# Loading the context's weights from ScalarE's queue, a unit behind each expert's tanh, and sharing the units out by the experts' rows

## The chip, the cores and the metric

One core of a Trainium2 chip runs one program. The time is that of the device in microseconds (us); the kernel before took 2759.27 us, the median of three runs from 2755.33 to 2763.97.

## The reference

Two models run one after the other on 256 tokens of width 1024, in float32. The first is one layer: attention, then 32 experts of which each token takes four. The second has two layers of attention, gated MLP, convolution and feed-forward, and besides its own tokens it carries a context of 256 tokens through its first layer. Cut to what matters here:

```
def moe_ffn(h, ...):                      # first model
    top_val, top_idx = lax.top_k(h @ w_router + b_router, 4)
    for each expert e and the tokens that chose it:
        gu  = x @ w_gate_up[e] + b_gate_up[e]             # 1024 -> 2048
        g   = minimum(gu[:, :1024], 7); u = clip(gu[:, 1024:], -7, 7)
        act = (u + 1) * (g * sigmoid(1.702 * g))
        y  += gate * (act @ w_down[e] + b_down[e])        # 1024 -> 1024
x = first_block(x, ...)
for l in range(2):                        # second model
    k_all = concatenate([kc, k]); ...     # the latent attends to the context too
    x = layer(x, k_all, v_all)
    if l == 0:
        xc = layer(ctx, kc, vc)           # the context, same weights, needs no x
```

The context's layer reads nothing that the first model computes, so it can be worked on while the experts run.

## The kernel before

**Experts.** An expert has 12.6 MB of weights. They are loaded in tiles of 2 MB, four for `w_gate_up` (L947) and two for `w_down` (L958), by SP's queue, into a ring of three such tiles (`big`, L930ff). The experts have fixed capacities, handed out by load: one of 128 rows, 15 of 64, 16 of 32 (`CAPS`). `GROUPS` sets their order: groups of four of 32 rows and of two of 64 take turns, with the one of 128 in between; from the eighth group on only pairs of 64 are left. For a group the tokens are gathered on PE (L847, into `hG`); for each expert follow the biases (L1036), the up matmuls (L981), `swiglu` (L915ff: clip on VectorE, tanh on ScalarE at L923 into `et`, two products on VectorE into `eg`), the transposes (L987), ScalarE's copy into `aT` (L989), the down matmuls (L1006) and ScalarE's copy into `y` (L1042). The down matmuls of an expert are emitted behind the up matmuls of the next. `combine` spreads a group's result over the tokens (L897, L898; L903 adds it to `xT`).

**The context pass.** `ctx_pass` (L1416ff) is a generator: between two `yield`s it emits about one unit. A unit is one block of weights of 1024 × 512 (2.1 MB, `load_w`, L317ff), fetched in four loads of 512 KB at L330 into three buffers `raws` and, every fourth, `rawx`; eight splits into a high and a low part (ScalarE `whis` L342, VectorE `wlos` L343), and 96 matmuls at L365 into the banks `side`. It ends with a residual (L1728, L1729) and a store of 1 MB to DRAM on GpSimd's queue (`cd`, L1570). While `self.side` is true the tiles are the context's own.

**What sets the order.** A scheduler orders each engine's instructions by priority. `prio` (L1765ff) emits the experts at high priority; after each of their `yield`s it lets `run_ctx(n)` emit n steps of the context at low priority. `MOE` holds these n: one in two of three entries for 22 entries, then one in each. When the context has ended, `self.solo` becomes true, and from there `big` may hand out five more tiles of 1 MB (`SPARE`), which were the context's.

**The seam.** Behind the last expert all engines branch on whether a token was left over (`overflow`, L1070ff; it is not taken here), and the second model's layers begin, with ScalarE's squares of `xT` into `merged` (L238).

Of the kernel before, what the change touches and what calls it, by code (L numbers as in the profile page):

```python
# [14 lines left out]
AF = mybir.ActivationFunctionType  # L15
# [12 lines left out]
CAPS = [128] + [64] * 15 + [32] * 16  # L28
SEQ = list(range(16, 20)) + [1, 2] + list(range(20, 24)) + [3, 4] + list(range(24, 28)) + [0] + list(range(28, 32)) + list(range(5, 16))
GROUPS = [[]]  # L30
# [68 lines left out]
class Builder:  # L99
    def __init__(self, tc, a, out, dbg=None):  # L100
        self.tc, self.nc, self.a, self.out = tc, tc.nc, a, out
        self.dbg = dbg or {}
        self.n = self.slot = self.hslot = 0
        self.side = False
        self.fbg = 0
        self.nblock, self.second = 0, None
        self.firstw = []
        self.after, self.fill = None, deque()
        self.cq = {False: deque(), True: deque()}
        self.cpool, self.cpool_s = CPOOL, CPOOL_S  # L110
        self.bg = deque()
# [204 lines left out]

    def load_w(self, w, q=None):

        q = q or self.nc.sync
        small = self.side  # L320
        if self.tail:
            self.nblock += 1
            small = self.nblock % 3 == 0
        whole = None if small else self.t(self.raw, [P, 4096], tag="raw")
        rows, k0 = [], 0
        for h in (1, 1, 1, 1) if small else (2, 2):
            n = 2 * h
            r = self.half() if small else whole[:, k0 * 512:(k0 + n) * 512]
            r = r.rearrange("p (k n) -> p k n", k=n)
            q.dma_start(r, w[:, k0:k0 + n, :])  # L330
            rows += [r[:, i:i + self.wn, :] for i in range(0, n, self.wn)]
            k0 += n
        return rows
# [583 lines left out]
    def swiglu(self, pool, pg, pu, n):  # L917
        nc = self.nc
        g = self.t(pool, [P, 512], tag="eg", bufs=1)
        nc.vector.tensor_scalar(g[:, :n], pg[:, :n], 7.0, None, op0=OP.min)  # L920
        nc.vector.tensor_scalar(pu[:, :n], pu[:, :n], -7.0, 7.0, op0=OP.max, op1=OP.min)
        th = self.t(pool, [P, 512], tag="et", bufs=1)
        nc.scalar.activation(th[:, :n], g[:, :n], AF.Tanh, scale=0.5 * 1.702)  # L923
        nc.vector.scalar_tensor_tensor(g[:, :n], th[:, :n], 1.0, g[:, :n], op0=OP.add, op1=OP.mult)
        nc.vector.scalar_tensor_tensor(g[:, :n], pu[:, :n], 1.0, g[:, :n], op0=OP.add, op1=OP.mult)
        return g
# [839 lines left out]
    def build(self, stop=None):  # L1766
        tc, a = self.tc, self.a
        with ExitStack() as st:
# [6 lines left out]
            with tc.tile_pool(name="ps1", bufs=1, space=PSUM) as self.psum, \  # L1775
# [5 lines left out]
                def run_ctx(n):  # L1781
                    self.side = True
                    for _ in range(n):
                        if next(ctx, 1):
                            self.solo = True
                            break
                    self.side = False
# [6 lines left out]
                with tc.tile_pool(name="moe", bufs=1) as mp:  # L1794
# [5 lines left out]
                    with tc.tile_pool(name="mw", bufs=1) as self.mw:  # L1800
                        self.prio(self.moe(mp), MOE, run_ctx)
                        run_ctx(100)
# [34 lines left out]
TSLOTS = ("gl", "gate")  # L1837
FRONT = [2, 2, 2, 1, 1, 1, 1, 1, 1, 1, 1, 1, 1, 1, 1, 1, 1, 1]
ROUTE = [1, 0, 0]
MOE = [1 if i % 3 else 0 for i in range(22)] + [1] * 22  # L1840


_BIG = ['w_ada', 'w_in', 'w_out', 'b_router', 'w_gate_up', 'b_gate_up', 'w_down', 'b_down', 'ada_w_2', 'w_in_2',
# [37 lines left out]
```

## Time and profile before

| | |
|---|---|
| median of three runs | 2759.27 us |
| profiled execution, its own time | 2754.71 us |
| its span | 2752.8 us |
| PE busy in the span | 2592.5 us (94%) |
| VectorE / ScalarE / GpSimd busy | 1626.1 / 1157.5 / 322.2 us |
| moved in all | 769.80 MB, mean 280 GB/s |
| first and last tanh of the experts | 349.1 and 1561.7 us |

PE is TensorE's matmul queue, PEld its weight loads, DVE VectorE, ACT ScalarE, POOL GpSimd, SP the engine whose queue issues most loads; a q behind a name is the engine's sequencer, which waits and issues. A row of the table of windows gives a stretch in us from the span's start, its length, then busy us and (x) number of instructions of PE, PEld, DVE, ACT and POOL, the granted clock of PE as a share of full speed, the share of time in which the DMA engines are busy, and GB/s. A row of waits gives who waits (engine, tile, line), for whom, the us in total, how often, and the longest. A row of a timeline gives start, us, engine, line, operation, out<-in, and in brackets how long the engine stood idle before and who released it. Names of weights read as in the program (`in_w_ff_dram` are the feed-forward weights).

### The profile page before, as it was taken

The numbers are of one execution on the slowest core, as the hardware profiler recorded it, in microseconds if no ns is written. First come the engines' busy times: TensorE is split into PE (matmuls) and PEld (weight loads), VectorE is DVE, ScalarE is ACT, GpSimd is POOL, SyncE is SP. The second block draws the span as 40 slices with busy tenths as digits, with TensorE's granted clock in tenths as the row PEclk, the third lists the DMA queues.
The fourth block names the chain that finished last, engine by engine and source line by source line (L and its number), as shares of the span: only waits on it lengthen the run. The fifth ranks groups of instructions, "written<-read, shape, count | busy, mean of one in ns | idle before, by whom it ended". The sixth has DMA issues, their size and how long they took to land. (4 is left out here: it accounts for less than half of the span.)

```text
span 2752.8 us, 49781 instructions
## 1 busy us (share of the span) xinstructions
PE 2592.5 (94%) x20358; PEld 2047.0 (74%) x20359; DVE 1626.1 (59%) x3090; ACT 1157.5 (42%) x1987; POOL 322.2 (12%) x334
## 2 busy tenths in 40 slices
PE   7999999999899999999889978899999998999998
PEld 5657877678567777875333477899789987899998
DVE  3465543778554524443121279988546789996655
ACT  2333343333243323431111156765445566656543
POOL 0000000000000000000000025442001055350000
PEclk9989899999999999999999989999999999999999
DMA  9758599989999999999999934326854443344442
GB/s 398 300 226 296 203 401 417 364 347 405 378 357 386 390 361 361 409 419 363 392 392 421 415 129 168 125 105 238 289 203 184 158 180 123 131 146 184 154 184 85
DMA packets 119370, 769.80 MB, mean 280 GB/s; under 512 B 11632, under 2 KB 12016, under 8 KB 52832
## 3 DMA queue, kind: packets, MB, share of 16 engines
q1 hardware_dynamic: 117744, 759.15, 70.6%
q0 software_dynamic: 1392, 7.41, 0.7%
q8 instruction: 162, 2.65, 0.4%
q14 instruction: 72, 0.59, 0.1%
HBM read 762.84 MB, written 3.67 MB: 278 GB/s over the span
## 5 line engine op out<-in xcount | busy, mean ns | idle before, releaser
L343 DVE TENSOR_TENSOR wlo<-raw,whi 128x1024 fp32r<-128x1024 f32 (+1 forms) x288 | 337.6, 1175 | 162.2 <-ACT whi L342 156.6
L365 PE MATMUL lin<-hhi,wlo 128*128 128x256 f32 x1440 | 399.3, 283 | 21.6 <-DVE wlo L343 21.6
L365 PE MATMUL lin<-hhi,whi 128*128 128x256 f32 x1440 | 400.5, 282 | 2.2 <-ACT hhi L284 2.2
L365 PE MATMUL lin<-hlo,whi 128*128 128x256 f32 x1440 | 401.4, 281 | 0.1
L342 ACT ACTIVATE whi<-raw 128x1024 fp32r<-128x1024 f32 (+1 forms) x288 | 276.9, 963 | 257.9 <-PE lin L365 189.3
L981 PE MATMUL mlin<-raw,hG 128*32 128x256 f32 (+2 forms) x2920 | 341.3, 456 | 17.5 <-DMA raw<-in_w_gate_up_dram 17.5
L365 PEld LDWEIGHTS lin<-hhi,wlo 128*128 128x128 f32 x1440 | 269.5, 190 | 37.5 <-DVE wlo L343 33.2
L1585 POOL TENSOR_TENSOR yc<-yc,ctmp 128x256 f32<-128x256 f32 x240 | 252.4, 1075 | 300.6 <-ACT ctmp L1584 300.1
L343 DVE TENSOR_TENSOR wlos<-raws,whis 128x512 fp32r<-128x512 f32 x246 | 166.2, 687 | 196.3 <-ACT whis L342 189.4
L365 PEld LDWEIGHTS lin<-hhi,whi 128*128 128x128 f32 x1440 | 271.0, 189 | 5.8 <-ACT hhi L284 3.7
L365 PEld LDWEIGHTS lin<-hlo,whi 128*128 128x128 f32 x1440 | 272.2, 189 | 3.7 <-issue 2.3
L981 PEld LDWEIGHTS mlin<-raw,hG 128*32 128x32 f32 (+2 forms) x2920 | 129.9, 121 | 178.6 <-issue 110.0
L342 ACT ACTIVATE whis<-raws 128x512 fp32r<-128x512 f32 x246 | 148.9, 627 | 225.6 <-PE side L365 186.2
L365 PE MATMUL side<-hhi,whis 128*128 128x256 f32 x720 | 203.0, 288 | 0.1
L365 PE MATMUL side<-hlo,whis 128*128 128x256 f32 x720 | 199.7, 282 | 0.0
L365 PE MATMUL side<-hhi,wlos 128*128 128x256 f32 x720 | 193.1, 284 | 0.7 <-DVE wlos L343 0.5
L343 DVE TENSOR_TENSOR wlo<-raws,whi 128x1024 fp32r<-128x1024 f32 x108 | 139.0, 1287 | 74.4 <-ACT whi L342 73.8
L1587 DVE SCALAR_TENSOR_TENSOR yc<-gl,cw,yc 128x256 f32<-128x256 f32 x240 | 167.8, 734 | 0.1
L342 ACT ACTIVATE whi<-raws 128x1024 fp32r<-128x1024 f32 x108 | 114.4, 1059 | 118.8 <-PE lin L365 103.8
L1006 PE MATMUL main<-raw,aT 128*32 128x256 f32 (+2 forms) x1408 | 162.6, 453 | 1.1 <-DMA raw<-in_w_down_dram 1.0
L365 PEld LDWEIGHTS side<-hhi,whis 128*128 128x128 f32 x720 | 136.7, 190 | 16.5 <-issue 11.2
L365 PE MATMUL lin<-ahi,whi 128*128 128x256 f32 x528 | 145.7, 279 | 0.0
(603 smaller groups left out, 5737.4 us busy)
## 6 DMA issues: line engine op xcount, KB each, us to landing
raw<-in_w_gate_up_dram SPq DMA_DIRECT2D x120, 2048.0 KB, 11.5
raw<-in_w_down_dram SPq DMA_DIRECT2D x55, 2048.0 KB, 11.1
raw<-in_w_in_dram SPq DMA_DIRECT2D x60, 1024.0 KB, 7.1
raws<-in_w_in_dram SPq DMA_DIRECT2D x95, 512.0 KB, 6.8
raws<-in_w_ff_dram SPq DMA_DIRECT2D x88, 512.0 KB, 8.1
raw<-in_w_ff_dram SPq DMA_DIRECT2D x44, 1024.0 KB, 7.0
phi<-in_ada_w_dram SPq DMA_DIRECT2D x10, 1024.0 KB, 7.4
plo<-in_ada_w_dram SPq DMA_DIRECT2D x10, 1024.0 KB, 7.1
```

What stands on the lines that cost most here:

```text
L342: x = nc.scalar.activation(flat(hi), flat(rows[i]), AF.Copy)
L343: y = nc.vector.tensor_sub(flat(lo), flat(rows[i]), flat(hi).bitcast(F32))
L365: x = nc.tensor.matmul(*args, skip_group_check=True, **kw)
L981: nc.tensor.matmul(d, hT(k), gu[k][c0 // D][:, c0 % D:c0 % D + W], start=False, stop=(k == KC - 1), skip_group_check=True)
L1006: nc.tensor.matmul(pys[h][g * C:(g + 1) * C, :W], st, dn[m][:, c0:c0 + W], start=(m == 0), stop=(m == KC - 1), skip_group_check=True)
L1585: nc.gpsimd.tensor_add(d, d, m)
L1587: self.paced(1, nc.vector.scalar_tensor_tensor(d, x, wcol, d, op0=OP.mult, op1=OP.add))
```

## The change

The loads of a unit of the context are issued by ScalarE's queue in place of SP's. `swiglu` keeps its tanh in `self.eload`, and the first of a unit's four loads is ordered behind the tanh that was emitted last. `MOE` is computed: each expert earns context steps by its capacity, 1.3 for 32 rows, 0.55 for 64, 0 for 128; a step is handed out when the sum reaches a whole number. What remains is emitted behind the last expert by `run_ctx(100)`. In all 164 loads go to ScalarE's queue, and since the context now ends behind the last expert, `solo` is not true in any expert: the five tiles of 1 MB aren't used for expert weights. Line numbers behind the change are 2 higher.

```diff
--- before.py
+++ after.py
@@ -104,7 +104,7 @@
         self.side = False
         self.fbg = 0
         self.nblock, self.second = 0, None
-        self.firstw = []
+        self.firstw, self.eload = [], None
         self.after, self.fill = None, deque()
         self.cq = {False: deque(), True: deque()}
         self.cpool, self.cpool_s = CPOOL, CPOOL_S
@@ -316,7 +316,7 @@
 
     def load_w(self, w, q=None):
 
-        q = q or self.nc.sync
+        q = q or (self.nc.scalar if self.side else self.nc.sync)
         small = self.side
         if self.tail:
             self.nblock += 1
@@ -327,7 +327,9 @@
             n = 2 * h
             r = self.half() if small else whole[:, k0 * 512:(k0 + n) * 512]
             r = r.rearrange("p (k n) -> p k n", k=n)
-            q.dma_start(r, w[:, k0:k0 + n, :])
+            x = q.dma_start(r, w[:, k0:k0 + n, :])
+            if self.side and self.eload is not None and k0 == 0:
+                self.behind(x, self.eload)
             rows += [r[:, i:i + self.wn, :] for i in range(0, n, self.wn)]
             k0 += n
         return rows
@@ -920,7 +922,7 @@
         nc.vector.tensor_scalar(g[:, :n], pg[:, :n], 7.0, None, op0=OP.min)
         nc.vector.tensor_scalar(pu[:, :n], pu[:, :n], -7.0, 7.0, op0=OP.max, op1=OP.min)
         th = self.t(pool, [P, 512], tag="et", bufs=1)
-        nc.scalar.activation(th[:, :n], g[:, :n], AF.Tanh, scale=0.5 * 1.702)
+        self.eload = nc.scalar.activation(th[:, :n], g[:, :n], AF.Tanh, scale=0.5 * 1.702)
         nc.vector.scalar_tensor_tensor(g[:, :n], th[:, :n], 1.0, g[:, :n], op0=OP.add, op1=OP.mult)
         nc.vector.scalar_tensor_tensor(g[:, :n], pu[:, :n], 1.0, g[:, :n], op0=OP.add, op1=OP.mult)
         return g
@@ -1837,7 +1839,22 @@
 TSLOTS = ("gl", "gate")
 FRONT = [2, 2, 2, 1, 1, 1, 1, 1, 1, 1, 1, 1, 1, 1, 1, 1, 1, 1]
 ROUTE = [1, 0, 0]
-MOE = [1 if i % 3 else 0 for i in range(22)] + [1] * 22
+SHARE = {32: 1.3, 64: 0.55, 128: 0.0}
+
+
+def moe_steps():
+
+
+    steps, due, done = [], 0.0, 0
+    for group in GROUPS:
+        for i in [None] + group:
+            due += SHARE[CAPS[i]] if i is not None else 0.0
+            steps.append(int(due) - done)
+            done = int(due)
+    return steps
+
+
+MOE = moe_steps()
 
 
 _BIG = ['w_ada', 'w_in', 'w_out', 'b_router', 'w_gate_up', 'b_gate_up', 'w_down', 'b_down', 'ada_w_2', 'w_in_2',
```

**ScalarE, among the late experts of 64 rows.** Before, behind the tanh into `et` (L923), only the experts' own copies stand:

```order
L923 ACTIVATE et_12493<-eg_12490 128x512 [waits DVE_49,Activation_49]
L989 ACTIVATE aT_12502<-main_12497 128x512 [waits PE_49]
L1042 ACTIVATE y_11574<-main_12508 64x512 [waits PE_49]
L1042 ACTIVATE y_11574<-main_12508 64x512
L290 ACTIVATE yh_12527<-y_11574,gcol_11572 128x512 [waits Activation_49]
L290 ACTIVATE yh_12545<-y_11574,gcol_11572 128x512 [waits DVE_49,PE_49]
L923 ACTIVATE et_12763<-eg_12760 128x512 [waits DVE_49]
```

Now loads of the context (L330, with the buffers that they fill) and its splits (`whis`) stand between an expert's tanh and its copy into `aT`:

```order
L290 ACTIVATE yh_12929<-y_12432,gcol_12430 128x512 [waits Activation_49]
L290 ACTIVATE yh_12947<-y_12432,gcol_12430 128x512 [waits DVE_49,PE_49]
L925 ACTIVATE et_13025<-eg_13022 128x512 [waits DVE_49]
L330 DMA raws_13061<-in_w_ff_2_dram 128x1024 [waits DMAHW4_49]
L330 DMA raws_13063<-in_w_ff_2_dram 128x1024 [waits DMAHW5_49]
L330 DMA raws_13065<-in_w_ff_2_dram 128x1024 [waits DMAHW6_49]
L991 ACTIVATE aT_13034<-main_13029 128x512 [waits PE_49]
L344 ACTIVATE whis_13071<-raws_13061 128x512 [waits DMAHW4_49]
L344 ACTIVATE whis_13087<-raws_13061 128x512
```

Three loads and, behind the copy into `aT`, the first two splits came in.

**VectorE, behind the last expert.** Before, the last additions of `combine` (L903) stand right ahead of the overflow check (L1070):

```order
L903 SCALAR_TENSOR_TENSOR xT_70<-main_14458,mod_14_97,xT_70 128x256 [waits DVE_49,PE_49]
L903 SCALAR_TENSOR_TENSOR xT_70<-main_14458,mod_14_97,xT_70 128x256 [waits DVE_49]
L903 SCALAR_TENSOR_TENSOR xT_70<-main_14465,mod_14_97,xT_70 128x256 [waits DVE_49,PE_49]
L903 SCALAR_TENSOR_TENSOR xT_70<-main_14465,mod_14_97,xT_70 128x256 [waits DVE_49]
L1070 TENSOR_LOAD ovi_5203 [waits DVE_49,DMASW1_49,PE_49,DMASW3_49,Activation_49,Pool_49]
L1071 COMPARE_AND_BRANCH
```

Now the context's last square root (`rs_`, nine instructions) and its residual into the tile `m` (L1730, L1731) stand between the last addition (L905) and the check (L1072):

```order
L905 SCALAR_TENSOR_TENSOR xT_70<-main_14377,mod_14_97,xT_70 128x256 [waits PE_49]
L905 SCALAR_TENSOR_TENSOR xT_70<-main_14377,mod_14_97,xT_70 128x256
L163 TENSOR_SCALAR rs_vs_14409<-side_14384 128x2 [waits PE_49]
...
L173 SCALAR_TENSOR_TENSOR rs_rs_14411<-rs_ts_14412,rs_rs_14411 128x2 [waits DVE_49]
L1730 SCALAR_TENSOR_TENSOR hks_14424<-y_1727_9377,Lp_208_1035,side_14421 128x256 [waits PE_49]
L1730 SCALAR_TENSOR_TENSOR hks_14427<-y_1727_9377,Lp_208_1035,side_14421 128x256
L1731 TENSOR_TENSOR m_1676_9091<-m_1676_9091,hks_14424 128x256 [waits DVE_49]
L1731 TENSOR_TENSOR m_1676_9091<-m_1676_9091,hks_14427 128x256 [waits DVE_49]
...
L1731 TENSOR_TENSOR m_1676_9091<-m_1676_9091,hks_14442 128x256 [waits DVE_49]
L1072 TENSOR_LOAD ovi_5203 [waits DVE_49,DMASW1_49,PE_49,DMASW3_49,Activation_49,Pool_49]
L1073 COMPARE_AND_BRANCH
```

The context's end moved from the middle of the experts to behind the last.

**GpSimd, at the context's store.** Before, the store `cd` (L1570) stands between two experts' `pick`s, seven experts ahead of the check:

```order
L1020 CAST pick_12712<-sel_5192 128x256 [waits PE_49,Pool_49]
L1570 DMA cd_2398_13739<-m_1704_9383 128x2048 [waits DMASW2_49,DVE_49]
L1020 CAST pick_13142<-sel_5192 128x256 [waits PE_49,Pool_49]
...
L1020 CAST pick_14290<-sel_5192 128x256 [waits PE_49,Pool_49]
L1070 TENSOR_LOAD ovi_5203 [waits DVE_49,DMASW1_49,PE_49,DMASW3_49,Activation_49,Pool_49]
L1071 COMPARE_AND_BRANCH
...
L1071 UNCONDITIONAL_BRANCH [waits Pool_sequencer_49]
```

Now it stands behind the check and its branches (L1073):

```order
L1022 CAST pick_13796<-sel_5192 128x256 [waits PE_49,Pool_49]
L1022 CAST pick_14064<-sel_5192 128x256 [waits PE_49,Pool_49]
L1072 TENSOR_LOAD ovi_5203 [waits DVE_49,DMASW1_49,PE_49,DMASW3_49,Activation_49,Pool_49]
L1073 COMPARE_AND_BRANCH
...
L1073 UNCONDITIONAL_BRANCH [waits Pool_sequencer_49]
L1572 DMA cd_2519_14448<-m_1676_9091 128x2048 [waits DMASW2_49,DVE_49]
```

The store moved from beside the experts to behind the branch. ScalarE's first instruction there (`merged` from `xT`, L238) lies in the memory of the tile `m` that the store reads; its list of waits, which has no store in the kernel before, now begins with the semaphore of this one. On SP's queue only the experts' loads are left in the middle stretch.

## Rows read from the trace of the kernel before

**Rows 1.** Windows: stretch, length, busy PE, PEld, DVE, ACT, POOL; PEclk; DMA share; GB/s.

```profile
349.00:934.00 585.00, 563.81 (x5026) 416.39 (x5025) 345.51 (x774) 213.50 (x419) 8.04 (x17) 0.98 0.96 381
934.00:1240.00 306.00, 305.44 (x2761) 237.00 (x2760) 126.20 (x223) 107.70 (x198) 2.91 (x7) 1.00 0.97 391
1240.00:1562.00 322.00, 287.46 (x1488) 131.39 (x1487) 69.10 (x146) 39.65 (x69) 3.74 (x9) 0.98 0.98 396
1562.00:1594.00 32.00, 21.68 (x100) 10.28 (x100) 11.11 (x24) 6.05 (x11) 0.10 (x1) 0.88 0.78 320
```

**Rows 2.** Windows of line L365 alone, the context's matmuls: PE and PEld.

```profile
934.00:1240.00 306.00, 171.31 (x1343) 160.77 (x1342) 1.00 0.97 391
1240.00:1562.00 322.00, 12.44 (x96) 11.50 (x95) 0.98 0.98 396
```

**Rows 3.** Timeline of POOL: the context's store is issued.

```profile
1276.09 0.54 POOL L1570 DMA_DIRECT2D cd<-m  x1 [28.92 <-DVE m L1729]
```

**Rows 4.** Waits of PE, 349 to 934 us: for weights.

```profile
PE mlin L981 <- DMA raw<-in_w_gate_up_dram: 5.9, 2, 4.3
```

**Rows 5.** Waits of PE, 934 to 1240 us: the only row.

```profile
PE mlin L981 <- DMA raw<-in_w_gate_up_dram: 0.5, 1, 0.5
```

**Rows 6.** Waits of PE, 1240 to 1562 us.

```profile
PE mlin L981 <- DMA raw<-in_w_gate_up_dram: 11.1, 7, 4.1
PE main L987 <- DVE eg L925: 7.1, 5, 1.5
PE mlin L1036 <- DVE eg L925: 5.9, 4, 1.5
PE main L897 <- ACT yh L290: 5.5, 4, 2.1
PE main L897 <- ACT m L290: 2.4, 2, 2.1
PE main L1006 <- DMA raw<-in_w_down_dram: 1.0, 1, 1.0
PE side L200 <- DVE sqs L254: 0.8, 1, 0.8
```

**Rows 7.** One window, the last four experts' loads.

```profile
1450.00:1562.00 112.00, 103.39 (x502) 48.88 (x498) 19.80 (x38) 13.11 (x23) 0.40 (x1) 0.98 1.01 421
```

**Rows 8.** The chain that ended last: one block of weights, 96 matmuls.

```profile
2060.30 11.10 PE lin L365 x96
```

**Rows 9.** Line L330 on SP's queue, 340 to 1600 us: ns min/median/max.

```profile
L330 SPq DMA_DIRECT2D raws<-in_w_ff_dram x48: 327/328/418, 865.5 to 1226.7; - x48
```

**Rows 10.** Waits of ACT, 349 to 1562 us: ahead of the tanh.

```profile
ACT et L923 <- DVE eg L920: 197.6, 29, 19.8
```

**Rows 11.** Timeline of PE at the seam: the last two combines.

```profile
1573.85 1.00 PE L897 MATMUL main<-G,m 128*128 128x256 f32 x3 [2.05 <-ACT m L290]
...
1586.02 1.20 PE L897 MATMUL main<-G,m 64*128 64x256 f32 x3 [1.92 <-ACT m L290]
```

**Rows 12.** Timeline of DVE: first and last of the context's last root.

```profile
1261.18 0.15 DVE L163 TENSOR_SCALAR rs_vs<-side 128x2 f32<-128x2 f32 x1
...
1265.05 0.16 DVE L173 SCALAR_TENSOR_TENSOR rs_rs<-rs_ts,rs_rs 128x2 f32<-128x2 f32 x1
```

**Rows 13.** Groups on DVE, 1268 to 1277 us: the context's last residual.

```profile
L1728 DVE SCALAR_TENSOR_TENSOR hks<-y,Lp,side 128x256 f32<-128x256 f32 x8 | 3.4, 470 | 0.0
L1729 DVE TENSOR_TENSOR m<-m,hks 128x256 f32<-128x256 f32 x8 | 3.0, 414 | 0.0
```

**Rows 14.** DMA issues: GpSimd's two stores of 1 MB, us to landing.

```profile
h2d<-raw POOLq DMA_DIRECT2D x1, 1024.0 KB, 6.9
...
cd<-m POOLq DMA_DIRECT2D x1, 1024.0 KB, 13.0
```

**Rows 15.** Timeline of ACT: the second model's first instruction.

```profile
1593.82 1.67 ACT L238 ACTIVATE merged<-xT 128x512 f32<-128x512 f32 x3 [7.24 <-PEq L1071]
```

**Rows 16.** Waits of SP's queue, 349 to 1562 us: ahead of L330.

```profile
SPq L330 <- DVE wlos L343: 302.8, 118, 6.4
```

## What the change will do, predicted before it was run

> **What bounds the kernel now.** I read the table of windows first, because the change only touches the stretch in which the 32 experts of the first model and the context pass of the second share the chip. I cut it at four tanhs: at the first (349 us), the fifteenth (934), the twenty-third (1240) and the last (1562), and then 32 us to the start of the second model's own layers. [rows 1] shows three different limits. From 349 to 934 PE is busy 563.8 of 585 us: PE bound, with DMA at 381 GB/s. From 934 to 1240 PE is busy 305.4 of 306: PE bound without a gap. From 1240 to 1562, ten experts of 64 rows, PE is busy only 287.5 of 322 and DMA has a share of 0.98.
>
> The same table for the matmuls of the context alone [rows 2] says why: 171.3 us of PE's middle stretch are context, 12.4 us of the late one. The context pass runs out at about 1276 us (its store is issued there, [rows 3]) and the last experts have nothing to be mixed with.
>
> Then PE's waits, stretch by stretch. Early, 5.9 us for expert weights [rows 4]; middle, 0.5 [rows 5]; late, 12.1 us for weights (11.1 + 1.0) and 21.7 us (7.1 + 5.9 + 5.5 + 2.4 + 0.8) for VectorE and ScalarE between an expert's steps [rows 6]. The ceiling of the one queue, SP's, is in [rows 7]: 421 GB/s over 112 us at a DMA share of 1.01. So the late stretch is bounded by DMA, with little room under it.
>
> **The change part by part.** It has three parts: the 164 context loads go from SP's queue to ScalarE's; the first load of each unit (96 matmuls, 2.1 MB) is ordered behind the tanh of the expert ahead; and the list of steps is shared out by rows, so that context work moves from the middle to the late stretch. The order of PE's instructions gives the counts. Context matmuls before and after: first fifteen intervals 2444 and 2464, next eight 1338 and 791, last ten 58 and 489, behind the last expert's tanh 0 and 96. One unit takes 11.10 us [rows 8], so a matmul is 0.1156 us.
>
> *Early stretch.* Same work, PE bound. SP issues less between expert loads, so some of the 5.9 us of waiting may go. I take half: −3. Bounds: −15 (all 21 us of PE's idle time but 6 filled) to +10 (if the new order of the loads opens gaps as large as half those).
>
> *Middle stretch.* It loses 547 matmuls: 547 × 0.1156 = 63 us, and PE would need 306 − 63 = 243. But bytes go too, fewer in proportion: 306 us × 391 GB/s = 119.6 MB, less 547/96 = 5.7 units of 2.1 MB = 11.9, leaves 107.7 MB, and at the ceiling of 421 GB/s these need 256 us. DMA becomes the bound. I take 306 − 256 = −50. Bounds: −63 (PE's 243) and −31 (bandwidth stays at 391: 275 us). It is nearer to the 421 of [rows 7], where DMA was also the bound.
>
> By the Trainium skill, "DMA: Bandwidth & Descriptors", section "Issuing engines are not separate DMA queues", loads issued by different engines run on the same DMA engines, and more issuers only save issue time. [rows 1] has a DMA share of 0.97 from one issuer, which fits; no row has two. If a second queue did add bandwidth, the middle would come down to PE's 243, and the sum 13 lower.
>
> *Late stretch.* PE's own work is 287.5 us, and 431 matmuls come in (489 − 58): 431 × 0.1156 = 49.8, so 337.3. The 21.7 us of waits for VectorE and ScalarE stay, since a unit lands in every second expert and then in one lump; the 12.1 us of DMA waits go, because DMA no longer bounds: 322 × 396 = 127.5 MB, plus 431/96 × 2.1 = 9.4, is 136.9 MB, 325 us at 421. PE with its waits needs 337.3 + 21.7 = 359. So +37. Bounds: +16 (all 21.7 filled by the new matmuls) and +50 (the DMA waits stay also). What hid the DMA so far was that, with the context ended, its five spare tiles of 1 MB took expert weights; now the context keeps them, and only the ring of three 2 MB tiles stands ahead of PE: 6 MB, 15 us at 421. If that cover fails, the 12 us come back.
>
> *Issue cost on ScalarE.* A load takes 0.33 us of the issuing queue [rows 9]; 164 × 0.33 = 54 us. ScalarE is busy 361 us of the 1213 before the last tanh [rows 1], and stands idle ahead of the tanh for 6.8 us on average (197.6 / 29, [rows 10]). Hidden, if the issue doesn't wait: 0, and rival C has the case that it does. On SP the same instructions go away.
>
> *The seam.* This is new. The last unit and the context's final residual and store now stand behind or beside the last expert. First, its 96 matmuls: 11.1 us on PE, less the holes that they fill there, 2.05 + 1.92 [rows 11]: +7. Second, on VectorE the context's last square root and residual stand behind the last combine: its nine small instructions took from 1261.18 to 1265.21, 4.0 us [rows 12], the residual 3.4 + 3.0 [rows 13]: 10.4. Third, the store to DRAM of the context is issued by GpSimd behind the branch of the overflow check, and ScalarE's first instruction of the next layer (merged from xT, which took over the stored tile's memory) waits for it. A 1 MB store from GpSimd took 6.9 us and, the same store under full load, 13.0 [rows 14]. DMA's share falls to 0.78 at the seam [rows 1], so 6.9. Before, that instruction started at 1593.82, released by the overflow check's branch [rows 15]; the branch's own cost stays. Seam: 7 + 10.4 + 6.9 = +24. Bounds: 14 (unit hidden wholly, the root finished beside the combine, store 6.9: 6.4 + 6.9) and 35 (nothing filled, store 13.0).
>
> *Sum.* −3 − 50 + 37 + 24 = +8. On the profiled execution, 2754.71 us (its span is 2752.8, 1.9 lie around it), that is 2763; the median of the runs shown is 2759.27, 4.6 more, so the forecast there is 2767. Nothing after the seam changes. The sum is a small difference of large terms: the 50 us taken from the middle come back in the late stretch and at the seam.
>
> **Rivals.** A measurement of this kernel tells from no change what differs by over 0.3%, 8.3 us: below 2751.0 is faster, above 2767.6 slower.
>
> *B, faster: the lumps fill the holes.* If the late experts' 21.7 us of waits are covered by context matmuls standing ready, late is +16, and if the seam comes at its lower bound, +14, the sum is −3 − 50 + 16 + 14 = −23: 2736. With only one of the two it is near −10; I take 2741 for the case. For it: in the middle, where the context is dense, the same kinds of waits are gone: 0.5 us in all [rows 5]. Against: there it has some 170 matmuls in each expert, late 49, in every second one.
>
> *C, slower: a load on ScalarE stands ahead of an expert's step.* A context load waits until VectorE has read the buffer that it fills. On SP these waits were 302.8 us in 118, 2.6 each [rows 16]. On ScalarE, a load that waits holds up all that is queued behind it: in the order shown for the late experts, three loads stand between a tanh and the copy of aT which the down matmuls wait for. If ten of the 32 experts lose 2.6 us so, it is +26 on top of the forecast: 2793. It decides from the point at which such a wait is longer than the 1.4 us (7.1 / 5) for which PE waits at the transposes already [rows 6]. For it: the length of SP's waits. Against: the loads' buffers are mostly read one unit ahead, and the tanh itself gates them.
>
> *D, slower: bandwidth doesn't rise.* If two queues interleave 512 KB and 2 MB loads without reaching the ceiling, the middle stays at 391 GB/s and takes 275 us, +19: 2786. For it: early and middle, with context loads between the experts', ran at 381 and 391, the pure stretch at 421 [rows 1, 7]. Against: early and middle were bounded by PE.
>
> **How the numbers follow.** Forecast 43%, B 30%, C 15%, D 12%. The forecast's own spread (early −15 to +10, seam +14 to +35) runs from 2745 to 2780, and its middle lies at the edge of slower: of its 43 I give 8 to faster, 19 to same, 16 to slower. B gives 26 to faster and 4 to same; C 14 to slower and 1 to same; D 12 to slower. In all faster 0.34, same 0.24, slower 0.42. The range reaches below B's 2736 by the early stretch's −15, to 2722, and above C's 2793 by +10, to 2802; with the unknown bounds of middle and late beyond it I leave 2 in 10 out.
>
> **What would show each step.** In the middle, PE's share falls below 0.97 and DMA runs near 421 GB/s, PE waiting for raw from w_gate_up; if instead PE stays full there, the bound was PE and the sum lower. Late, PE is busy about 337 us and its waits for weights nearly vanish. At the seam, ScalarE's first merged from xT has the context's store, or GpSimd, as its releaser, some 24 us later than the last tanh's 32 us. ScalarE's loads should show no waits above 1 us ahead of a tanh or aT. The prediction is wrong if the early stretch moves by more than 15 us, if SP's ring of three tiles starves PE late, or if the store is not waited for.

## The result: slower by 2.4%

The changed kernel took 2820.79 us (median of four runs, 2809.56 to 2824.5) against 2757.3: a ratio of 1.0237, with an interval of 1.0212 to 1.0261. Forecast were 2767, in a range to 2802. The direction was right; the size was not: +64 us in place of +8.

The windows of the changed kernel, cut at the same four tanhs (columns as in [rows 1]; the last one runs to the second model's first squares):

```profile
348.40:953.00 604.60, 575.72 (x5073) 426.82 (x5070) 349.02 (x793) 218.79 (x426) 9.23 (x17) 0.96 0.93 370
953.00:1242.80 289.80, 258.06 (x2210) 179.54 (x2209) 88.01 (x159) 74.96 (x139) 2.92 (x7) 0.95 0.91 366
1242.80:1604.40 361.60, 333.13 (x1887) 169.74 (x1885) 95.36 (x169) 68.57 (x116) 3.22 (x8) 0.99 0.96 378
1604.40:1662.00 57.60, 37.37 (x233) 24.97 (x231) 29.15 (x65) 13.97 (x23) 2.32 (x6) 0.84 0.60 229
```

Against [rows 1], and from the last tanh to the end of the span (2752.8 − 1561.7 before, 2822.4 − 1604.4 after):

| stretch | before | after | forecast | measured |
|---|---|---|---|---|
| early, 1st to 15th tanh | 585.0 | 604.6 | −3 | +20 |
| middle, to the 23rd | 306.0 | 289.8 | −50 | −16 |
| late, to the last | 322.0 | 361.6 | +37 | +40 |
| behind the last tanh | 1191.1 | 1218.0 | +24 | +27 |

The measured column is read from one profiled execution of each kernel. These two lie 70 us apart, which is what the column adds up to; the medians lie 64 apart.

Two terms, late and seam, held; two, early and middle, did not. The middle row is the one to read: PE is busy 258 of 290 us and DMA 0.91 of the time. Neither is full. Before, PE was.

The context's matmuls alone (L367 now), middle and late, answer to [rows 2]:

```profile
953.00:1242.80 289.80, 100.89 (x792) 94.61 (x791) 0.95 0.91 366
1242.80:1604.40 361.60, 67.64 (x527) 62.82 (x527) 0.99 0.96 378
```

So the work moved as the order said. (The forecast's 791 and 489 are counted in the order of instructions; by time, some 40 matmuls more fall behind the cut.) PE's waits in the middle, where [rows 5] had a single row of 0.5 us:

```profile
PE mlin L983 <- DMA raw<-in_w_gate_up_dram: 15.1, 7, 4.2
PE main L989 <- DVE eg L927: 6.3, 5, 3.0
PE main L1008 <- DMA raw<-in_w_down_dram: 5.5, 4, 4.1
PE main L899 <- ACT yh L290: 3.1, 2, 2.4
```

and late, answering to [rows 6]:

```profile
PE main L899 <- ACT yh L290: 11.5, 8, 2.5
PE main L989 <- DVE eg L927: 7.5, 5, 1.9
PE mlin L1038 <- DVE eg L927: 6.1, 4, 1.7
PE mlin L983 <- DMA raw<-in_w_gate_up_dram: 2.8, 4, 1.3
```

Late, the waits for weights fell from 12.1 to 2.8 us and those for VectorE and ScalarE stayed (25 us for 22), as forecast. In the middle PE now waits 20.6 us for weights although DMA is idle for a tenth of the time.

So this is how 63 us less work became 16 us less time. PE waits 31.5 us in place of 0.5: the 20.6 for weights, and 10.9 for VectorE and ScalarE (1.5 of it in rows too small to show). And the 243 us of work that are left keep PE busy for 258, since the granted clock is 0.95: 258 × 0.95 is 245.

Where DMA's idle time lies, five windows of 5 us behind the expert of 128 rows show:

```profile
1055.00:1060.00 5.00, 5.00 (x24) 4.94 (x24) 1.14 (x3) 0.60 (x1) 0.00 (x0) 0.50 0.83 349
1060.00:1065.00 5.00, 5.00 (x22) 2.17 (x20) 0.87 (x3) 0.00 (x0) 0.00 (x0) 0.99 0.00 0
1065.00:1070.00 5.00, 5.00 (x55) 2.69 (x58) 0.69 (x1) 0.00 (x0) 0.00 (x0) 1.00 0.00 0
1070.00:1075.00 5.00, 3.23 (x60) 2.75 (x52) 0.81 (x5) 0.38 (x1) 0.00 (x0) 1.00 0.84 301
1075.00:1080.00 5.00, 2.58 (x28) 1.21 (x31) 0.00 (x0) 0.00 (x0) 0.00 (x0) 0.72 1.04 442
```

and the timeline of SP's queue over it, then three rows of PE's:

```profile
1036.90 33.18 SPq L949 DMA_DIRECT2D raw<-in_w_gate_up_dram  x4
```

```profile
1043.62 1.08 PE L989 MATMUL main<-cst,eg 128*128 128x128 f32 x4 [3.05 <-DVE eg L927]
...
1051.59 0.50 PE L899 MATMUL main<-G,yh 128*128 128x256 f32 x2 [2.42 <-ACT yh L290]
...
1077.42 3.48 PE L983 MATMUL mlin<-raw,hG 128*32 128x256 f32 x32 [4.18 <-DMA raw<-in_w_gate_up_dram]
```

For 10 us nothing moves. The issue of four loads stretched over 33 us, the last one standing at 1069.7, since the ring's tiles are taken until PE has read them, and PE is behind with combine and gather. Then PE runs out of weights and stands for 4.2 us. The granted clock was 0.50, the lower of its two levels (1.2 GHz), from 1055 to 1060, behind gaps on PE of 3.1 and 2.4 us.

The seam (DVE, POOL, ACT: the residual's last step, the store, the first squares), answering to [rows 12, 13, 15]:

```profile
1644.83 0.16 DVE L163 TENSOR_SCALAR rs_vs<-side 128x2 f32<-128x2 f32 x1
...
1653.98 0.42 DVE L1731 TENSOR_TENSOR m<-m,hks 128x256 f32<-128x256 f32 x1 [1.01 <-DVEq L1073]
...
1654.71 0.54 POOL L1572 DMA_DIRECT2D cd<-m  x1 [149.64 <-DVE m L1731]
...
1659.54 1.67 ACT L238 ACTIVATE merged<-xT 128x512 f32<-128x512 f32 x3 [18.51 <-DMA cd<-m]
```

Root and residual take 9.6 us, the squares wait for the store, 4.8 us from its issue: the two steps forecast at 10.4 and 6.9. From the last tanh to these squares it is 55.1 us, 32.1 before: 23 us for the 24 forecast. The other 4 of the row's 27 lie behind the squares, where the kernels of this series take between 1156 and 1167 us, whatever their seam.

### The profile page after: what moved, and what is told of

It reads as the page before. It is cut to its first block, busy times and chain, and to the rows that moved or that the text cites. A ratio compares the mean times of both kernels' runs of the same rounds, so it can differ in the third digit from the quotient of the medians.

```text
span 2822.4 us, 49492 instructions
## 1 busy us (share of the span) xinstructions
PE 2617.3 (93%) x20358; PEld 2054.1 (73%) x20359; DVE 1629.6 (58%) x3090; ACT 1162.7 (41%) x1987; POOL 323.8 (11%) x334
## 5 line engine op out<-in xcount | busy, mean ns | idle before, releaser
L367 PE MATMUL lin<-hhi,wlo 128*128 128x256 f32 x1440 | 399.8, 283 | 19.4 <-DVE wlo L345 19.2
L983 PE MATMUL mlin<-raw,hG 128*32 128x256 f32 (+1 forms) x3040 | 378.4, 468 | 27.8 <-DMA raw<-in_w_gate_up_dram 27.6
L367 PE MATMUL lin<-hhi,whi 128*128 128x256 f32 x1440 | 401.8, 282 | 2.2 <-ACT hhi L284 2.2
L367 PE MATMUL lin<-hlo,whi 128*128 128x256 f32 x1440 | 402.4, 281 | 0.0
L367 PEld LDWEIGHTS lin<-hhi,wlo 128*128 128x128 f32 x1440 | 270.9, 190 | 34.2 <-DVE wlo L345 29.9
L983 PEld LDWEIGHTS mlin<-raw,hG 128*32 128x32 f32 (+1 forms) x3040 | 136.9, 122 | 202.4 <-issue 124.2
L367 PEld LDWEIGHTS lin<-hhi,whi 128*128 128x128 f32 x1440 | 273.0, 191 | 6.5 <-ACT hhi L284 4.4
L367 PEld LDWEIGHTS lin<-hlo,whi 128*128 128x128 f32 x1440 | 274.0, 190 | 3.2 <-issue 1.4
L367 PE MATMUL side<-hhi,whis 128*128 128x256 f32 x720 | 202.3, 287 | 1.1 <-ACT hhi L284 1.1
L367 PE MATMUL side<-hlo,whis 128*128 128x256 f32 x720 | 199.2, 282 | 0.0
L1008 PE MATMUL main<-raw,aT 128*32 128x256 f32 (+2 forms) x1536 | 190.4, 470 | 5.8 <-DMA raw<-in_w_down_dram 5.5
L367 PE MATMUL side<-hhi,wlos 128*128 128x256 f32 x720 | 191.0, 284 | 0.7 <-DVE wlos L345 0.4
L344 ACT ACTIVATE whi<-raws 128x1024 fp32r<-128x1024 f32 x108 | 114.5, 1060 | 122.3 <-PE lin L367 101.1
L367 PEld LDWEIGHTS side<-hhi,whis 128*128 128x128 f32 x720 | 136.9, 190 | 16.2 <-issue 13.8
L1022 POOL CAST pick<-sel 128x288 fp32r<-128x288 f32 (+1 forms) x32 | 16.2, 508 | 1138.5 <-PE mlin L1038 1089.5
## 6 DMA issues: line engine op xcount, KB each, us to landing
raws<-in_w_ff_dram ACTq DMA_DIRECT2D x48, 512.0 KB, 11.5
```

What stands on the lines that cost most here:

```text
L344: x = nc.scalar.activation(flat(hi), flat(rows[i]), AF.Copy)
L367: x = nc.tensor.matmul(*args, skip_group_check=True, **kw)
L983: nc.tensor.matmul(d, hT(k), gu[k][c0 // D][:, c0 % D:c0 % D + W], start=False, stop=(k == KC - 1), skip_group_check=True)
L1008: nc.tensor.matmul(pys[h][g * C:(g + 1) * C, :W], st, dn[m][:, c0:c0 + W], start=(m == 0), stop=(m == KC - 1), skip_group_check=True)
L1022: nc.gpsimd.tensor_copy(pick.rearrange("p (c n) -> p c n", c=n), src.unsqueeze(2).to_broadcast([P, n, w]))
```

## The experiments

All stand against runs of the kernel before on the same chip; the ratio is given as its 95% interval. The stretches are those of one profiled execution each, tanh to tanh; the counts are context matmuls by the instruction order, middle / late. The kernels of e10 ran once each, and their total, longer by the context left for the end, says nothing.

| run | what it is | median us | ratio to before | matmuls | early | middle | late | behind |
|---|---|---|---|---|---|---|---|---|
| – | before | 2757.3 | | 1338 / 58 | 585.4 | 305.3 | 322.0 | 1191.1 |
| – | changed | 2820.8 | 1.0212–1.0261 | 791 / 489 | 604.5 | 289.9 | 361.6 | 1218.0 |
| e1 | SP's queue, new shares, no ordering | 2776.3 | 1.0076–1.0118 | 1350 / 11 | 596.3 | 313.1 | 318.5 | 1194.9 |
| e2 | ScalarE's queue, ordering, old list | 2827.0 | 1.0248–1.0301 | 759 / 777 | 595.4 | 279.6 | 406.7 | 1198.3 |
| e3 | ScalarE's queue, new shares | 2791.8 | 1.0126–1.0160 | 1365 / 11 | 600.1 | 321.5 | 322.2 | 1203.7 |
| e4 | ScalarE's queue, old list | 2776.7 | 1.0058–1.0103 | 1358 / 36 | 604.8 | 312.0 | 316.8 | 1192.9 |
| e5 | SP's queue, ordering, new shares | 2803.5 | 1.0149–1.0183 | 791 / 489 | 594.0 | 286.3 | 356.9 | 1218.2 |
| e6 | before without spare tiles | 2762.6 | 1.0019–1.0059 | 1338 / 58 | 584.5 | 304.7 | 331.5 | 1194.5 |
| e8 | changed, last unit one expert earlier | 2823.0 | 1.0228–1.0265 | 791 / 585 | 604.0 | 287.3 | 394.5 | 1187.9 |
| e9 | changed, 2.0 steps for 128 rows | 2786.9 | 1.0091–1.0125 | 983 / 393 | 602.7 | 292.9 | 357.3 | 1195.8 |
| e10 | changed, no context from the eighth interval on | | | 0 / 0 | | 240.4 | 326.5 | |
| e11 | changed, first units on SP's queue | 2818.1 | 1.0206–1.0264 | 744 / 536 | 597.6 | 290.1 | 363.5 | 1214.7 |
| e12 | e9 on SP's queue | 2794.0 | 1.0131–1.0186 | 992 / 384 | 594.9 | 286.2 | 368.0 | 1190.2 |
| e13 | e6, late units behind tanhs | 2800.5 | 1.0136–1.0196 | 628 / 768 | 585.2 | 266.9 | 402.1 | 1198.4 |
| e14 | e6, ScalarE's queue from the 15th tanh | 2772.6 | 1.0056–1.0105 | 1338 / 58 | 580.4 | 313.2 | 334.5 | 1193.8 |

**Which part of the change does it (e1 to e5).** Each takes parts out of the changed kernel. In e1 and e5 the loads go back to SP's queue:

```diff
-        q = q or (self.nc.scalar if self.side else self.nc.sync)
+        q = q or self.nc.sync
```

In e1, e3 and e4 the ordering behind the tanh is left out:

```diff
-            if self.side and self.eload is not None and k0 == 0:
-                self.behind(x, self.eload)
```

In e2 and e4 the list of steps is the old one:

```diff
-MOE = moe_steps()
+MOE = [1 if i % 3 else 0 for i in range(22)] + [1] * 22
```

e1: 

> The new shares alone: loads stay on SP's queue, no ordering behind the tanh. The instruction order puts the context's matmuls where they were before (first fifteen intervals 2479, next eight 1350, last ten 11, behind the last tanh 0), only the five spare tiles are no longer used. Theory P (the slow-down comes from where the context's work now stands): early and middle stretch as before (585 and 306 us, each within 5), no seam cost (1191 us behind the last tanh, within 5), late stretch 322 to 334 (the 12 us of weight waits can come back): 2757 to 2770. Theory S (the shares themselves do the damage): 2800 or more.

e2: 

> ScalarE's queue and the ordering behind the tanh, with the old list of steps: by the instruction order the context still is thinned in the middle (759 matmuls) and moved late (777), but ends three experts ahead of the last. Theory P: early and middle as in the changed kernel (+19 and -15 against before), late +35 to +45, no seam cost: 2790 to 2805. Theory S: as before, 2757.

e3: 

> The changed kernel without the ordering behind the tanh: ScalarE's queue, new shares. Matmuls stand as before (2464, 1365, 11, 0). Theory Q (a load issued from ScalarE holds up the experts' copies): early stretch +10 to +20 against before, total 2770 to 2785 with the lost spare tiles. Theory P: the queue costs nothing by itself, time as the kernel with the new shares alone on SP, within 5 us.

e4: 

> ScalarE's queue alone: no ordering behind the tanh, the old list of steps. Matmuls stand as before (2446, 1358, 36, 0), spare tiles used. Theory Q: +10 to +20 against before. Theory P: as before within 5 us.

e5: 

> The changed kernel with the context's loads back on SP's queue; the ordering behind the tanh and the new shares stay, and so do the counts of context matmuls per stretch (2464, 791, 489, 96). Theory P (placement): as the changed kernel, 2810 to 2825. Theory Q (the queue is worth about 15 to 25 us by itself, as the two kernels without the ordering say: 2776 to 2792 with the new shares): 2795 to 2808.

The counts already say that the shares alone move nothing: without the ordering behind the tanh the scheduler fills PE with context as early as before (e1, e3, e4), with it the work comes late under either list (e2, e5). So it is the ordering that thins the middle. By the ratios' middles, each difference times 2757 us, it costs 26 us under the new shares (e3, 1.0143, to changed, 1.0237) and 54 under the old list (e4, 1.0080, to e2, 1.0275, which has the wait of e8 below in it). The queue costs 13 (e1, 1.0097, to e3), 20 (e5, 1.0166, to changed) and 22 us (before to e4). These three prices hold the queue and a new order together: where the queue changes, the scheduler also places 2797 to 3342 of the 8399 matmuls ahead of the overflow check otherwise.

Of these five expectations only e5's theory Q held outright. Theory P for e2 fell 22 us short of the 2827.0; theory Q fell 7 us short for e3 and 2 for e4 (10 to 20 us, where it was 22). e1 missed its 2757 to 2770 by 6: in the early stretch PE waited 8.8 us at once for a convolution's sum on VectorE, a wait that e5 has too (7.8), and before not (0.6):

```profile
PE side L1629 <- DVE y L1587: 8.8, 1, 8.8
```

**The spare tiles (e6).**

```diff
-        spare = len(SPARE) if solo else 0
+        spare = 0
```

> The kernel before, but the five spare tiles are never used for expert weights; the instruction order on PE is the same. Theory R (the lost spare tiles are what the new shares alone cost, 25 us): 2770 to 2780, and the loss in the late stretch. Theory N (the new shares alone cost through another fine order in the early and middle stretch, where that kernel lost 11 and 8 us): the late stretch stays at 322 within 5 and the total at 2751 to 2760.

Late +9.5, in all a ratio of 1.0039, 11 us: the total, 2762.6, lies between the two theories. The spare tiles are worth something, not the 27 us of e1; the new list's other cost is the early and middle stretch of e1. The last four intervals, first the kernel before, then e6:

```profile
1442.40:1561.70 119.30, 109.44 (x530) 51.47 (x528) 21.57 (x40) 14.04 (x24) 0.80 (x2) 0.99 1.01 421
```

```profile
1441.10:1569.90 128.80, 109.51 (x528) 45.43 (x528) 21.39 (x40) 14.03 (x24) 0.80 (x2) 1.00 0.94 388
```

The 421 GB/s of [rows 7], on which the forecast of the middle rests, were reached with the spare tiles: from 1440 to 1562 us 22 of the 36 expert loads went into them, in the middle none of 42. With the ring of three alone the same experts get 388.

**The seam and the gap (e8, e9).**

e8 hands two steps out earlier:

```diff
 MOE = moe_steps()
+MOE[-4] += 1
+MOE[-2] += 1
```

e9 changes one number:

```diff
-SHARE = {32: 1.3, 64: 0.55, 128: 0.0}
+SHARE = {32: 1.3, 64: 0.55, 128: 2.0}
```

e8: 

> The changed kernel with its last unit of context, its residual and its store placed one expert earlier; else the same order. The store then stands ahead of the overflow check and ScalarE's first instruction behind it no longer waits for it. My seam term: the stretch behind the last tanh falls from 1218 by 24, to 1191 to 1197, and the last expert's interval grows by the unit's 11 us less holes: total -10 to -20 against the changed kernel, 2800 to 2810. If the seam's cost were the clock or the branch: 1215 or more stays.

e9: 

> The changed kernel with one number changed: the expert of 128 rows earns 2.0 steps in place of 0, so that its successor's interval (39.3 us, PE idle 9.8, half clock in parts, no context matmul) gets 164 context matmuls, and the context ends before the last expert. Theory G (the middle's loss is gaps without context work, into which the ring of three tiles runs empty): that interval grows by less than 10 us for 19 us of added work, the seam falls by 24, the total is 2780 to 2795. Theory B (bandwidth is the bound in the middle): that interval grows by 164 x 0.1156 = 19 us, only the seam is won: 2800 to 2810.

In e8 the way from the last tanh to the first squares fell from 55.1 to 32.0 us, the value before: the seam's mechanism is shown. (The whole stretch fell by 30; the other 7 lie behind the squares.) The total didn't fall and missed its 2800 to 2810, for a reason that I had not seen: the generator ended one expert earlier, so the last expert was given the spare tile `y8`, which the context's last residual still read. SP's loads stood for 16 us ahead of this one. PE's waits from 1590 us on:

```profile
PE mlin L983 <- DMA y<-in_w_gate_up_dram: 9.2, 1, 9.2
PE mlin L983 <- DMA raw<-in_w_gate_up_dram: 4.1, 1, 4.1
```

The last interval took 66 us in place of 41. e9 came out as theory G had it. It gave 34 us back by the medians; its profiled execution lies 27 below that of the changed kernel, 22 of them at the seam. The context matmuls that it adds to the middle, 192 or 22 us of PE, cost 3. The interval behind the expert of 128 rows, first the changed kernel, then e9, then the kernel before:

```profile
1041.40:1080.70 39.30, 29.50 (x262) 18.66 (x262) 8.03 (x19) 5.14 (x10) 0.00 (x0) 0.83 0.59 234
```

```profile
1039.90:1082.20 42.30, 39.53 (x399) 31.00 (x400) 19.70 (x38) 15.87 (x29) 0.21 (x1) 0.96 0.78 308
```

```profile
1033.80:1071.10 37.30, 37.30 (x436) 32.44 (x435) 21.45 (x42) 16.16 (x30) 0.00 (x0) 1.00 0.84 320
```

137 matmuls more for 3 us, and the granted clock rises from 0.83 to 0.96. Bandwidth was not the bound there. The kernel before did 174 matmuls more than the changed one there, in 2 us less.

**What an expert takes alone (e10).** All shares are 0:

```diff
-SHARE = {32: 1.3, 64: 0.55, 128: 0.0}
+SHARE = {32: 0.0, 64: 0.0, 128: 0.0}
```

and in a second kernel the ring has two tiles:

```diff
-        j = self.slot % (spare + 3)
+        j = self.slot % (spare + 2)
...
-        if j == spare:
-            return self.t(self.mw, [P, 2, 2048], tag="raw3")
```

e10: 

> All shares set to 0 in the changed kernel: from the eighth interval on no context matmul and no context load stands among the experts (27 units come behind the last one, so the total is some 300 us longer and says nothing). It shows what an expert takes alone, through a ring of three 2 MB tiles. Theory B (DMA bounds an expert without context): 12.6 MB at 421 GB/s, 29.9 us in each interval of 32 or 64 rows. Theory G (the ring runs empty and the steps of an expert wait for one another): 33 to 36 us for 32 rows, DMA at 350 to 385 GB/s, PE half clocked in parts; for 64 rows, late, 31 to 33.

The ring of two: 

> The same with a ring of two tiles in place of three. Theory G: the tiles set how far the loads run ahead, so an expert alone takes 3 us or more longer than with three, at a lower rate. Theory B: 29.9 us again.

With three tiles, an expert of 32 rows inside its group, one behind the expert of 128 rows, and the whole middle:

```profile
668.50:698.20 29.70, 17.59 (x205) 8.33 (x202) 1.61 (x4) 2.31 (x7) 0.40 (x1) 0.84 1.01 423
930.50:969.70 39.20, 28.27 (x262) 18.18 (x262) 8.04 (x19) 5.12 (x11) 0.00 (x0) 0.85 0.68 269
...
856.00:1096.30 240.30, 179.56 (x1418) 91.56 (x1418) 29.22 (x70) 23.10 (x52) 2.93 (x7) 0.87 0.91 370
```

With two, such an expert inside its group and the one behind 128 rows:

```profile
698.90:733.80 34.90, 17.89 (x206) 8.21 (x202) 1.62 (x4) 2.28 (x6) 0.40 (x1) 0.79 0.92 356
1011.90:1056.70 44.80, 29.85 (x262) 18.09 (x262) 8.04 (x19) 5.12 (x10) 0.00 (x0) 0.85 0.69 267
```

Each theory held in a place. Inside a group DMA is the bound, 29.7 us at 423 GB/s; most experts there take 28 to 33 us. Where a group begins, its first expert takes 33 to 39 us: the ring fills while PE combines and gathers, and behind the expert of 128 rows SP issued no load from 937.0 to 957.5. A tile less costs 5 us inside the group, 6 at its start. The middle so runs at 370 GB/s without any context work, which is what the changed kernel had, 366.

**The price of the move alone (e13), and of the queue alone (e11, e14, e12).**

e13 is e6 with the ordering for late units alone (`nsw` counts the tanhs emitted, `NSW` is 19):

```diff
+            if self.side and self.nsw >= NSW and k0 == 0:
+                self.behind(x, self.eload)
```

> The kernel before without the spare tiles (2762.6 us; 584.5, 304.7 and 331.5 in its three stretches), and only units emitted behind the nineteenth tanh are ordered behind an expert's tanh; all loads on SP's queue. Context matmuls per stretch: 2444 as before, 628 for 1338, 768 for 58, none behind the last. Theory M (what the runs so far say: a matmul taken from the middle gives back about 0.03 us, one added late costs about 0.08): early 585, middle 280 to 287, late 382 to 395, behind the last tanh 1191 to 1196, total 2788 to 2805. Theory F (my forecast's rule, the larger of PE's work and DMA at 421 GB/s, which would hold if the early stretch, the queue and the seam had spoilt it): middle 246 to 256, late 388 to 395, total 2755 to 2772.

The windows of e13, middle and late (e6 has 304.7 and 331.5, PE's clock at 1.00 and 0.98):

```profile
933.20:1200.00 266.80, 235.40 (x2059) 158.25 (x2057) 73.75 (x138) 63.88 (x121) 2.91 (x7) 0.96 0.95 387
1200.00:1602.10 402.10, 374.52 (x2186) 209.61 (x2184) 123.83 (x227) 84.73 (x144) 4.07 (x9) 0.98 0.90 356
```

710 matmuls, 82 us of PE's work, left the middle, which gave back 38 (0.053 us each), and came in late, where they cost 71 (0.099 each). The early stretch stayed at 585. The total is M's, the middle lies between M and F, and late came out 7 us above both (M had put 0.08 for a matmul). The move loses by itself, and part of the changed kernel's poor middle was its own.

e14 is e6 with the queue alone (`NSW` is 15), e11 the changed kernel with the first units on SP's queue:

```diff
-        q = q or self.nc.sync
+        q = q or (self.nc.scalar if self.side and self.nsw >= NSW else self.nc.sync)
```

```diff
-        q = q or (self.nc.scalar if self.side else self.nc.sync)
+        q = q or (self.nc.scalar if self.side and self.eload is not None else self.nc.sync)
```

and e12 is e9 with e5's first edit.

e11: 

> The changed kernel, but context loads that are emitted before the first expert's tanh stay on SP's queue; the later ones go to ScalarE's. In the changed kernel the first interval between tanhs takes 34.3 us, on SP's queue 26.7. If ScalarE's queue costs because these first loads overtake the first experts' weights: that interval is back at 26.7, the total -7 to -9 against the changed kernel, 2811 to 2815. If the queue costs throughout (loads held up in ScalarE's order): the first interval back, but the total within 5 of the changed kernel less 8 only by that.

e14: 

> The kernel before without the spare tiles; context loads emitted behind the fifteenth tanh go to ScalarE's queue, nothing is ordered behind a tanh, and the order of PE's matmuls is the same. If ScalarE's queue costs wherever it is used: middle and late stretch together 5 to 12 us longer than 636 (304.7 + 331.5). If its cost is that of the early stretch (first loads overtaking expert weights): 2762.6 within 4.

e12: 

> Both repairs together: context loads on SP's queue (worth 17 us against the changed kernel) and 2.0 steps for the expert of 128 rows (worth 33). If they add, 2766 to 2774, still slower than the kernel before by the spare tiles (7) and the new list's early stretch (9). If they overlap (both fill the same gaps), 2778 to 2790.

In e14 PE's order is that of e6 but for 16 of 8399 places, so that nearly the queue alone differs. It costs 12 us by the ratios (1.0081 against 1.0039; by their intervals some 3 to 20), as the first theory had it. Middle and late together are 11.5 us longer, of which the early stretch gives 4 back. PE's waits in its middle, where e6 has none:

```profile
PE mlin L984 <- DMA raw<-in_w_gate_up_dram: 7.8, 4, 2.6
```

e11 brings the first interval from 34.3 to 26.7 us and the early stretch down by 7, but the total hardly (ratio 1.0235); its interval is too wide to tell a gain of 7 us from none, so it decides between neither theory. e12 lies above both of its ranges, and the queue's sign is turned: on SP's queue the kernel is slower than e9, its interval lies above e9's, and late it has 368 us for 357. So the repairs don't add, and what the queue costs depends on the order that it meets, or comes in part from the new order that goes with it; why ScalarE's queue helps e9 was not found out.

## Why the prediction was wrong

*Middle, the step that failed.* I put its new length at the larger of PE's work and the bytes at 421 GB/s, 256 us. It took 290, at 366 GB/s. The 421 of [rows 7] comes from a stretch with the five spare tiles, which the middle never had; with three tiles it holds inside a group (423 in e10), not across the starts of groups (388 in e6's last four intervals). There the loads stop when PE stands at a group's start and PE stops when the loads have to catch up, so the stretch is longer than either: 240 us with no context at all (e10), where the rule gives 88 MB / 0.421 = 209. The context matmuls had been filling just these places. Taking 547 away gave 16 us, not 50; taken alone, 710 gave 38 (e13). The lower bound that I set, bandwidth at 391, was no bound, since it too let the loads run on.

Against the forecast's 256, which is 243 of work and 13 of waiting for weights, the missing 34 us are three terms: 8 more of waiting for weights, 11 of waiting for VectorE and ScalarE, which I had kept late but put at nothing here since the dense middle showed none, and 15 of PE's busy time, 258 us for a work of 243, with the granted clock down from 1.00 to 0.95.

*Early, the second step.* "Same work, PE bound" left out the fine order; it moved by +20, and a move of more than 15 us was one of my signs of being wrong. By its values in all runs: old list on SP's queue 584.5 to 585.4 (before, e6, e13), new shares on SP's queue 594.0 to 596.3 (e1, e5, e12), ScalarE's queue from the start 600.1 to 604.8 (e3, e4, e8, e9, changed). e2's 595.4 has 140 context matmuls, 16 us, less in it. So the list alone costs some 10 us (its sign is the wait of 8.8 us in e1), the queue alone 19 (e4), and both together 15 to 19: they don't add. Of the 20, 12 are PE's busy time (563.8 to 575.7, at a clock of 0.98 and 0.96) and 8 its idle time. Why the order costs this was not followed further; my upper bound was +10.

*Late and seam.* Right in size and by their steps: PE busy 333 us for the 337 forecast, weight waits nearly gone, engine waits kept; root and residual 9.6 us for 10.4, store 4.8 for 6.9, and 8.6 for the 7 of the unit. The direction, slower, came from these two terms.

*The range.* Its sums were a little off: by their own terms the forecast's spread ends at 2791, not 2780, C with the early bound at 2806, not 2802, and the lower end is 2724, not 2722. The measured 2820.79 lies outside either way.

*Rival C* named the queue, by loads that wait on ScalarE. Their issues are short in the changed kernel (ns min/median/max):

```profile
L330 ACTq DMA_DIRECT2D raws<-in_w_ff_dram x48: 334/380/678, 912.8 to 1605.4; - x48
L330 ACTq DMA_DIRECT2D raws<-in_w_in_dram x39: 334/334/335, 406.4 to 800.9; - x39
```

But these times hold no waiting, which shows as a gap in ScalarE's order, here one of 7.2 us:

```profile
1014.29 0.63 ACT L344 ACTIVATE whis<-rawx 128x512 fp32r<-128x512 f32 x1 [0.73 <-DVE wlos L345]
1022.07 0.33 ACTq L330 DMA_DIRECT2D rawx<-in_w_ff_dram  x1
```

Ahead of ScalarE's loads there are 78 such gaps of over 0.15 us from the first tanh to 1605 us, 105 us in all. So the loads did wait, as C had it. They did not hold up the steps that C named: every tanh started within 0.2 us of its input, every copy into `aT` within 0.6 (0.9 and 0.7 before). C's 26 us were not paid in that way.

ScalarE also waited for loads held behind the tanh: the splits of the feed-forward weights stand in its order and wait 57.9 us in all, in 17 places; before it was 13.7 in 5, in e3, without the ordering, 1.5 in 1:

```profile
ACT whis L344 <- DMA raws<-in_w_ff_dram: 57.9, 17, 8.2
```

That with ScalarE's queue expert weights come late because context loads no longer stand in line behind them, is argued from e14's 7.8 us and not shown further.

*Rivals B and D.* B's filling didn't come: late, 25 us of engine waits stayed. D's bandwidth of 391 was nearer than 421, and for a reason other than two queues: e10 has 370 without any context load.

## What to carry to other kernels

Where two streams share the engines through a small ring, don't price a stretch by the larger of its two totals: look for the places where each stops the other (here the start of a group), and run one stretch without the filler to see them. Take a ceiling of bandwidth only from a stretch with as many tiles. Filler work, done while the main work would wait, is free because of where it stands; spreading it evenly moves it away from the gaps, and here half (e13) to three quarters (the change) of its removed time came back as waiting and at a lower granted clock. And look at what stands last: work that ends behind the main path puts its whole tail, root, residual, store, on it.

## What the runs showed of the hardware

A second issuer brought no bandwidth. The middle of e14, with the context's loads on ScalarE's queue and the experts' on SP's, moved 386 GB/s at a DMA share of 0.96; e6, all on SP's, 390 (second row):

```profile
929.20:1242.40 313.20, 305.40 (x2760) 236.65 (x2760) 125.88 (x222) 107.28 (x197) 3.14 (x7) 1.00 0.96 386
```

```profile
933.80:1238.50 304.70, 304.70 (x2756) 236.38 (x2754) 125.55 (x221) 107.56 (x198) 2.93 (x7) 1.00 0.97 390
```

By the Trainium skill, "DMA: Bandwidth & Descriptors", section "Issuing engines are not separate DMA queues", this is to be expected, and there the gain is the issuer's time alone. In these runs it cost time: 12 us in e14, with nearly the same order of matmuls.
